# Scores on VectorE in one instruction per head, with paired score matmuls, a four-piece first weight unit and values by token tile

## The chip, the cores and the metric

The kernel runs on one core of a Trainium2 chip. The metric is the device time of one execution in microseconds (us), the median of several runs. The core has TensorE (PE, matrix products; PEld is its weight load), VectorE (DVE), ScalarE (ACT), GpSimd (POOL) and SyncE (SP), which issues the DMA transfers. Each engine works through its own instructions in order and waits on semaphores for the others.

## What is computed

A network of ten stages on 256 tokens of width 1024 in fp32: attention and MLP (layer 0), a state-space mixer and MLP (layer 1), and then twice a gated feed-forward, a mixer with differential attention and a causal convolution, and a second feed-forward. What the change touches is the softmax of the two attentions of layer 0 and of the two differential attentions. Cut to that:

```python
def windowed_gqa_sink(q, k, v, sink):       # attention "A": 8 query heads, 2 key heads
    s = einsum(qb, kb) * HEAD_DIM ** -0.5
    s = where(valid, s, NEG_INF)             # a band of 128 tokens
    p = softmax(concatenate([s, sink]))[..., :-1]
    return einsum(p, vb)

def neighborhood_attention(q, k, v, rpb):   # attention "B": 8 heads, a bias per head
    s = einsum(q_r, k_blk) * scale
    s = where(mask, s + bias, NEG_INF)
    return einsum(softmax(s), v_blk)

def diff_attention(q, k, v, rel_bias, lam, lam_init, subln_g):   # 4 heads x 2 maps, causal
    s = einsum(qi, k) * scale + bias
    p = softmax(where(dist >= 0, s, -1e30))
    a = p[:, :, 0] - lam * p[:, :, 1]
    return rms_norm(einsum(a, v), subln_g) * (1.0 - lam_init)
```

## The kernel before

The 256 tokens are two token tiles of 128 (`t` = 0, 1). Activations lie in SBUF in transposed form; an fp32 product is made of three fp32r matmuls, from a high part and a rest of both factors: names ending in `h` or `hh` are high parts, `l` or `hl` the rests. Only the key and value projections and the attention part of the output projection of the differential layers run as exact fp32 matmuls, straight from the weight buffer `st`. A matmul of fp32 operands (these, the scores `sc`, the products `po`) counts as two instructions in the trace. Weights come as 270 packed units of 1 MB through `unit` (L736) into three buffers `st`; ACT casts each half to `wh` (128x1024) and DVE subtracts to get `wl`. SP issues every transfer, in its order.

**The order.** The code does not issue its instructions directly. A `Recorder` keeps each operation with a priority (its number in the code plus the offsets of the table `BIAS` and of `rec.prio`), an estimated cost and its predecessors; `schedule` (L329) simulates the five engines and picks for each the ready operation of lowest priority; `issue` then writes all of them out from one line, L546, which is therefore the line of nearly every row of the trace. So an edit of a cost, of the order in the code or of the number of operations can move the instructions around it on every engine. Behind the scheduler each engine's order is fixed.

**The start.** `load_x` brings X in four pieces of 256 KB (token tile 0, columns 0 and 512; then tile 1), `first_T` transposes them (`tr<-ident,X`) to `xhl`, and `up` (L777) multiplies by the first unit (keys and values of A, `parts=FIRST_PARTS`, with `t_outer` all of tile 0 before tile 1). That unit is loaded in `FIRST_PARTS` = 2 pieces of 512 KB. `warm` runs 16 matmuls on a constant before.

**Attention of layer 0.** `attn` (L1153) runs `heads(t, part)` for part 0 (A) of both tiles, then, after the projections `up_T` for B, part 1 (B) of both tiles. `heads` calls `softmax_pair` (L1131) four times: for head pair (a, j) it takes a bank `sc`, computes two heads' scores with keys and queries on 64 partitions (rows 0 to 63 of the array for j = 0, rows 64 to 127 for j = 1), and then does, for both heads at once on DVE, `s = sc * 0.125 + bias` (SCALAR_TENSOR_TENSOR, 128x512), the maximum (TENSOR_REDUCE) and the negated maximum `nmx`; A's takes the minimum with `nsink` in the same small instruction. ACT makes exp with `nmx` as its bias per head and sums it; PE transposes the result (`tr<-ident,s`), which is copied to `pt` and multiplied by the values (`po`). A has 8 such pairs and B has 8. The acc rows beside B's scores are the output projection of A's result (`acc<-wh,hh` and so on).

**Differential layers.** `diff` works like that in its own `heads(t)`: four score banks for each tile, by (a, m), of two heads `u` each; tile 0 sees 128 keys (heads of 128x128), tile 1 sees 256. The three DVE steps per bank, exp on ACT, then on DVE `drd` (reciprocal), `dcc` and four `s<-s,dcc` that subtract the second map, transposes on PE (`ptps`), copies `pt`, products with the values `po`, a norm (`dss`, with a power on POOL, and `on`), transposes of `on`, copies `hd`, and the output projection `acc<-st,hd`. Beside all that DVE works off a causal convolution of 31 taps, the instructions `y<-ut,dprep,y` (120 of 128x256 per layer), whose result `hh`, `hl` is the other half of the output projection. The values are projected by `up([(W, 2048, 512)])`, 16 exact matmuls over the 8 slices of x, both tiles for each slice (`up<-st,x`).

Of the kernel before, what the change touches and what calls it, by code (L numbers as in the profile page):

```python
# [10 lines left out]
F32 = mybir.dt.float32  # L11
F32R = mybir.dt.float32r
AF = mybir.ActivationFunctionType
ALU = mybir.AluOpType
# [605 lines left out]
FIRST_PARTS = 2  # L620
# [59 lines left out]
class Net:  # L680
# [55 lines left out]
    def unit(self, srcs, a, exact=False, parts=1):  # L736
# [7 lines left out]
        for i in range(parts):  # L744
            nc.sync.dma_start(out=st[:, i * n:(i + 1) * n], in_=src[:, i * n:(i + 1) * n])
# [4 lines left out]
        for i in range(2):  # L750
# [5 lines left out]
            nc.scalar.copy(hv, s)  # L756
            nc.vector.tensor_tensor(lv, s, hv.bitcast(F32), op=ALU.subtract)
# [19 lines left out]
    def up(self, segs, t_outer=False, exact=False, parts=1):  # L777
# [20 lines left out]
        if t_outer:  # L798
            for t in range(2):
                for k in range(KM):  # L800
                    do(k, wk[k], t)
# [329 lines left out]
    def softmax_pair(self, t, a, j, q, k, bias, nmx, sums, nsink, s, pt):  # L1131

        nc = self.nc
        ps = self.bank([128, 2, T], "sc")
        pr = slice(64 * j, 64 * j + 64)
        for m in range(2):
            nc.tensor.matmul(ps[:, m], q[pr, 2 * a + m, t * 128:(t + 1) * 128], k(m)[pr], start=True, stop=True)
        nc.vector.scalar_tensor_tensor(s, ps, ATTN_SCALE, bias, op0=ALU.mult, op1=ALU.add)
        h2 = slice(4 * a + j, 4 * a + j + 3, 2)
        mx = self.tiny([128, 2], "mx")  # L1140
        nc.vector.tensor_reduce(mx, s, axis=AX.X, op=ALU.max)
        if nsink is not None:
            nc.vector.scalar_tensor_tensor(nmx[:, h2], mx, -1.0, nsink[:, h2], op0=ALU.mult, op1=ALU.min)
        else:
            nc.vector.tensor_scalar(nmx[:, h2], mx, -1.0, None, op0=ALU.mult)
        for m in range(2):
            h = 4 * a + j + 2 * m
            nc.scalar.activation(s[:, m], s[:, m], AF.Exp, bias=nmx[:, h:h + 1], accum_out=sums[:, h:h + 1])
# [4 lines left out]
    def attn(self, finish_of):  # L1153
        nc, I = self.nc, self.I
        W, Wo = Mat("attn_w_in", 0), Mat("attn_w_out", 0)
        with self.rec.phase_pool(name="attn", bufs=1) as ap:
# [18 lines left out]
            for t in range(2):  # L1175
                qn = nat()
                self.rope(ap, c, ps[t], 8, t, [qn.rearrange("p (h d) -> p h d", h=8)])
                self.transposes(qT[0][:, :, t * 128:(t + 1) * 128], qn, 4, nc.scalar.copy)

            def heads(t, part):  # L1180
# [3 lines left out]
                for a in range(2):  # L1184
                    s2 = self.w4([128, 2, 2, T], "s")
                    pt2 = self.w4([128, 2, 2, 2, 128], "pt")
                    for j in range(2):
                        if part == 0:
                            bias = c["band"][:, t].unsqueeze(1).to_broadcast([128, 2, T])
                            k = lambda m: kA[:, a]  # L1190
                        else:
                            e0 = 2 - 2 * t
                            bias = c["bt"][:, 4 * a + j:4 * a + j + 3:2, e0:e0 + 4].rearrange("p h e k -> p h (e k)")
                            k = lambda m: kB[:, 2 * a + m]
                        pt = self.softmax_pair(t, a, j, qT[part], k, bias, nmx, sums, c["nsink"] if part == 0 else None, s2[:, j], pt2[:, j])
# [653 lines left out]
```

## Time and profile before

| | |
|---|---|
| time, median of 3 runs | 1671.87 us (1671.65 to 1675.98) |
| the profiled execution | 1673.98 us |
| its span | 1672.2 us |
| PE busy | 1652.7 us (99%) |
| PEld busy | 1391.9 us (83%) |
| DVE busy | 1199.1 us (72%) |
| ACT busy | 924.0 us (55%) |
| POOL busy | 49.1 us (3%) |
| HBM read | 302.44 MB, 182 GB/s over the span |

The span is what the trace covers; 1.78 us of the profiled execution's time lie outside it. A row of the timeline gives the start, the time from first start to last end of a run of like instructions, the engine, the operation with its output and inputs, the shape, the count, and in brackets how long the engine had waited ahead of it and for what. Rows of successive instructions overlap a little, so the cost of an instruction in a chain is the distance from its start to the next start, and is smaller than its duration.

### The profile page before, as it was taken

The page shows a single profiled execution, that of the slowest core. Times are in us where ns is not written, and L with a number is a line of the kernel's source. Part 1 is how long each engine was busy: PE and PEld are TensorE (multiplying, and loading weights), DVE is VectorE, ACT ScalarE, POOL GpSimd, SP SyncE. Part 2 cuts the span into 40 slices and gives each one's busy share as a digit, 9 for nine tenths or more (in the row PEclk, how much of TensorE's full clock was granted, in tenths as well). Part 3 has the DMA queues.
Part 4 walks back from the last instruction along what each step waited for, and adds up shares of the span by engine and source line. Part 5 has one row for each costly group of instructions (what it writes and reads, how often), then busy time and mean ns, then how long its engine had stood idle before and what let it go on. Part 6 is the DMA issues. An engine that isn't in the chain of part 4 may idle for free.

```text
span 1672.2 us, 22864 instructions
## 1 busy us (share of the span) xinstructions
PE 1652.7 (99%) x8854; PEld 1391.9 (83%) x8854; DVE 1199.1 (72%) x1902; ACT 924.0 (55%) x1696; POOL 49.1 (3%) x50
## 2 busy tenths in 40 slices
PE   8999999999999999999999999999999999999999
PEld 7888888899987888888888658888888887578887
DVE  6767665999998666686665988665666658977652
ACT  5654444599995444465544257554455443566551
POOL 0000000000001000000000100000000001100000
PEclk9999999999999999999999999999999999999999
DMA  7535564384454556475554128555455532267540
GB/s 274 202 109 201 181 223 178 131 306 160 166 191 175 202 181 221 151 264 205 198 193 159 52 110 302 212 180 213 152 207 196 193 128 96 101 254 250 200 151 25
DMA packets 45694, 305.04 MB, mean 182 GB/s; under 512 B 5073, under 2 KB 5265, under 8 KB 11281
## 3 DMA queue, kind: packets, MB, share of 16 engines
q1 hardware_dynamic: 45584, 303.58, 49.8%
q8 instruction: 69, 1.13, 0.3%
q14 instruction: 41, 0.33, 0.1%
HBM read 302.44 MB, written 1.11 MB: 182 GB/s over the span
## 4 chain that ended last, share of the span: by engine, by line
PE 48%; DVE 7%; POOL 1%; issue 0%; ACT 0%; POOLq 0%; DVEq 0%
PE upW L546 24%; PE acc L546 17%; PE up L546 6%; DVE y L546 4%; PE tr L546 1%; POOL qr L546 1%; DVE s L546 1%; DVE dnmx L546 1%; DVE wl L546 0%; DVE X L546 0%; POOL rs L546 0%; DVE hn L546 0%; PE upT L546 0%; DVE nat L546 0%; PE ms L546 0%
## 5 line engine op out<-in xcount | busy, mean ns | idle before, releaser
L546 DVE TENSOR_TENSOR wl<-st,wh 128x1024 fp32r<-128x1024 f32 x516 | 623.0, 1219 | 220.4 <-PE upW L546 113.0
L546 ACT CAST wh<-st 128x1024 fp32r<-128x1024 f32 (+1 forms) x516 | 529.5, 1048 | 329.9 <-PE upW L546 167.5
L546 PE MATMUL upW<-xhl,wh 128*128 128x512 f32 x1600 | 403.4, 390 | 0.0
L546 PEld LDWEIGHTS upW<-xhl,wh 128*128 128x128 f32 x1600 | 297.5, 188 | 59.7
L546 PE MATMUL acc<-wh,hh 128*128 128x512 f32 x736 | 288.1, 394 | 0.0
L546 PE MATMUL acc<-wl,hh 128*128 128x512 f32 x736 | 287.5, 392 | 0.0
L546 PE MATMUL acc<-wh,hl 128*128 128x512 f32 x736 | 261.6, 392 | 0.0
L546 PE MATMUL up<-wh,xhl 128*128 128x512 f32 (+2 forms) x704 | 221.0, 386 | 3.6 <-ACT xhl L546 3.2
L546 PEld LDWEIGHTS upW<-xhl,wl 128*128 128x128 f32 x1600 | 205.3, 191 | 7.8
L546 PE MATMUL upW<-xhl,wl 128*128 128x256 f32 x1600 | 208.5, 283 | 0.0
L546 PEld LDWEIGHTS acc<-wh,hh 128*128 128x128 f32 x736 | 138.3, 188 | 29.0 <-issue 0.8
L546 PEld LDWEIGHTS acc<-wh,hl 128*128 128x128 f32 x736 | 138.2, 188 | 29.0 <-DVE hl L546 0.5
L546 PEld LDWEIGHTS acc<-wl,hh 128*128 128x128 f32 x736 | 138.5, 188 | 28.0 <-issue 1.4
L546 PEld LDWEIGHTS up<-wh,xhl 128*128 128x128 f32 x704 | 130.6, 190 | 28.7 <-ACT xhl L546 3.7
L546 PE MATMUL upT<-xhl,wh 128*128 128x256 f32 x736 | 138.9, 287 | 0.0
L546 PE MATMUL up<-wl,xhl 128*128 128x512 f32 (+2 forms) x352 | 136.1, 387 | 0.0
L546 PEld LDWEIGHTS upT<-xhl,wh 128*128 128x128 f32 x736 | 116.0, 191 | 1.6 <-issue 0.5
L546 PE MATMUL upT<-xhl,wl 128*128 128x256 f32 x368 | 104.9, 285 | 0.0
L546 DVE SCALAR_TENSOR_TENSOR y<-ut,dprep,y 128x256 f32<-128x256 f32 x240 | 98.5, 487 | 0.0
L546 PEld LDWEIGHTS up<-wl,xhl 128*128 128x128 f32 x352 | 66.7, 190 | 11.4
L546 PEld LDWEIGHTS upT<-xhl,wl 128*128 128x128 f32 x368 | 70.4, 191 | 0.3 <-issue 0.2
L546 DVE TENSOR_TENSOR r<-r,upW 128x256 f32<-128x256 f32 x56 | 23.2, 418 | 55.3 <-ACT r L546 55.3
(214 smaller groups left out, 1480.6 us busy)
## 6 DMA issues: line engine op xcount, KB each, us to landing
st<-in_pack SPq DMA_DIRECT2D x267, 1024.0 KB, 4.8
ar<-a_rows SPq DMA_DIRECT2D x16, 512.0 KB, 9.2
gv<-in_ln_g SPq DMA_DIRECT2D x4, 512.0 KB, 6.7
gv<-in_ln_b SPq DMA_DIRECT2D x4, 512.0 KB, 7.4
gv<-in_ffn_norm SPq DMA_DIRECT2D x4, 512.0 KB, 5.7
rpb_bt<-in_rpb_rows SPq DMA_DIRECT2D x1, 1536.0 KB, 8.0
st<-in_pack SPq DMA_DIRECT2D x2, 640.0 KB, 3.8
X<-in_x SPq DMA_DIRECT2D x4, 256.0 KB, 5.5
```

The source lines that it names most:

```text
L546: fn(*[real(a) for a in o.args], **{k: real(v) for k, v in o.kw.items()})
```

## The change

1. **Scores.** The three DVE steps of a pair become, for each head, one `tensor_tensor_reduce`: it writes `-(sc + bias)` to `s` and its minimum (in A together with the head's `nsink`) to `nmx`. The compiled program has two DVE instructions for it, `ISA s,nmx<-sc,...` of 128x256 (128x128 in tile 0 of the differential layers) and `ISA nmx` of 128x1, which fetches the accumulated value. Exp gets `scale=-1.0`. The factor 0.125 moves into the copies of the queries (an activation with a scale where a copy stood) and, in the differential layers, into `q_norm` (one tiny instruction per layer).
2. **Score pairs.** `scores` takes two banks and issues the score matmuls of a pair of banks alternately, one of row half 0, one of row half 1; `diff` does so as well.
3. **First unit.** `FIRST_PARTS` goes from 2 to 4: pieces of 256 KB, with priorities `FIRST_LATE`; casts and subtractions of this unit in halves (128x512); its matmuls by piece of two slices.
4. **Values by token tile.** In `diff` the values use `t_outer=True`, and the attention part of the output projection runs all of tile 0 and then all of tile 1.

PE's multiset of instructions stays the same; DVE goes from 1904 to 1940 instructions in the program, ACT from 1514 to 1516, SP from 319 to 321. The core of the diff:

```diff
-FIRST_PARTS = 2
+FIRST_PARTS = 4
+FIRST_LATE = (-45.5, -46.4, -46, -46)
...
         n = a * b // parts
         for i in range(parts):
-            nc.sync.dma_start(out=st[:, i * n:(i + 1) * n], in_=src[:, i * n:(i + 1) * n])
+            with self.rec.prio(FIRST_LATE[i] if parts > 1 else 0):
+                nc.sync.dma_start(out=st[:, i * n:(i + 1) * n], in_=src[:, i * n:(i + 1) * n])
...
-            nc.scalar.copy(hv, s)
-            nc.vector.tensor_tensor(lv, s, hv.bitcast(F32), op=ALU.subtract)
+            step = max(1, half // max(1, parts // 2))
+            for k in range(0, half, step):
+                ks = slice(k, k + step)
+                nc.scalar.copy(hv[:, ks], s[:, ks])
+                nc.vector.tensor_tensor(lv[:, ks], s[:, ks], hv[:, ks].bitcast(F32), op=ALU.subtract)
...
+        if parts > 1:
+            step = KM // parts
+            mm = self.nc.tensor.matmul
+            for t in range(2):
+                sl, o = slice(t * 128, (t + 1) * 128), ps[t][:, 0:n]
+                for k0 in range(0, KM, step):
+                    for p, (x, i) in enumerate(((self.xh, 0), (self.xl, 0), (self.xh, 1))):
+                        for k in range(k0, k0 + step):
+                            mm(o, x[:, k, sl], wk[k][i], start=k == 0 and p == 0, stop=k == KM - 1 and p == 2)
...
+    def scores(self, t, a, q, k):
+        pss = [self.bank([128, 2, T], "sc") for _ in range(2)]
+        for m in range(2):
+            for j, ps in enumerate(pss):
+                pr = slice(64 * j, 64 * j + 64)
+                self.nc.tensor.matmul(ps[:, m], q[pr, 2 * a + m, t * 128:(t + 1) * 128], k(m)[pr], start=True, stop=True)
+        return pss
...
-        nc.vector.scalar_tensor_tensor(s, ps, ATTN_SCALE, bias, op0=ALU.mult, op1=ALU.add)
-        h2 = slice(4 * a + j, 4 * a + j + 3, 2)
-        mx = self.tiny([128, 2], "mx")
-        nc.vector.tensor_reduce(mx, s, axis=AX.X, op=ALU.max)
...
         for m in range(2):
             h = 4 * a + j + 2 * m
-            nc.scalar.activation(s[:, m], s[:, m], AF.Exp, bias=nmx[:, h:h + 1], accum_out=sums[:, h:h + 1])
+            nc.vector.tensor_tensor_reduce(s[:, m], ps[:, m], bias[:, m], -1.0,
+                                           3e38 if nsink is None else nsink[:, h:h + 1], ALU.add, ALU.min,
+                                           accum_out=nmx[:, h:h + 1])
+            nc.scalar.activation(s[:, m], s[:, m], AF.Exp, bias=nmx[:, h:h + 1], scale=-1.0, accum_out=sums[:, h:h + 1])
...
-                self.transposes(qT[0][:, :, t * 128:(t + 1) * 128], qn, 4, nc.scalar.copy)
+                self.transposes(qT[0][:, :, t * 128:(t + 1) * 128], qn, 4,
+                                lambda o, p: nc.scalar.activation(o, p, AF.Copy, scale=ATTN_SCALE))
...
-                        nc.vector.scalar_tensor_tensor(sv, sc[:, :, 0:kn], ATTN_SCALE, self.t5[:, 2 * a:2 * a + 2, T - kn:T],
-                                                       op0=ALU.mult, op1=ALU.add)
-                        mx = nmx[:, m, 2 * a:2 * a + 2]
-                        nc.vector.tensor_reduce(mx, sv, axis=AX.X, op=ALU.max)
-                        nc.vector.tensor_scalar(mx, mx, -1.0, None, op0=ALU.mult)
                         for u in range(2):
                             h = 2 * a + u
-                            nc.scalar.activation(sv[:, u], sv[:, u], AF.Exp, bias=nmx[:, m, h:h + 1],
+                            mx = nmx[:, m, h:h + 1]
+                            nc.vector.tensor_tensor_reduce(sv[:, u], sc[:, u, 0:kn], self.t5[:, h, T - kn:T], -1.0, 3e38,
+                                                           ALU.add, ALU.min, accum_out=mx)
+                            nc.scalar.activation(sv[:, u], sv[:, u], AF.Exp, bias=mx, scale=-1.0,
                                                  accum_out=sums[:, m, h:h + 1])
...
-            ps = self.up([(W, 2048, 512)], exact=2 in EXACT_QKV)
+            ps = self.up([(W, 2048, 512)], t_outer=True, exact=2 in EXACT_QKV)
...
-            self.down(acc, self.items(hd, 4), Wo, True)
+            items = self.items(hd, 4)
+            ws = [w for i in (0, 2) for w in self.down_weights(Wo, items[i][2], items[i][0][1] is None)]
+            for t in range(2):
+                for i, ((h, k, _), w) in enumerate(zip(items, ws)):
+                    self.down_mm(acc, h, k, w, t, i == 0, False)
```

SP at the start; `st<-in_pack 128x1024` is a piece of 512 KB, `128x512` one of 256 KB, as is each X. Before:

```order
L546 DMA ident<-in_c_ident 128x128
L546 DMA X<-in_x 128x512 x2
L546 DMA st<-in_pack 128x1024 x2
L546 DMA X<-in_x 128x512 x2
L546 DMA st<-in_pack 128x2048 x2
L546 DMA asmall<-in_attn_small 128x648
```

After:

```order
L546 DMA ident<-in_c_ident 128x128
L546 DMA X<-in_x 128x512
L546 DMA st<-in_pack 128x512 x2
L546 DMA X<-in_x 128x512
L546 DMA st<-in_pack 128x512 x2
L546 DMA X<-in_x 128x512 x2
L546 DMA st<-in_pack 128x2048
L546 DMA asmall<-in_attn_small 128x648
```

The second piece of X now stands behind the first two pieces of the unit, and `asmall` (cosines, band, sink) ahead of the third unit instead of behind it. On PE the first `up` still comes behind eight transposes of X, that is behind both pieces of tile 0, but then as a run of nine of these matmuls instead of one.

PE in part A of the attention, from the scores on; `tr<-ident,s` are transposes of exp's result. Before:

```order
L546 MATMUL sc<-kA,qT_372 128x256 x4
L546 MATMUL tr<-ident,nat 128x128 x4
L546 MATMUL sc<-kA,qT_372 128x256 x12
L546 MATMUL upT<-xhl,wh 128x256
L546 MATMUL upT<-xhl,wl 128x256
```

After:

```order
L546 MATMUL sc<-kA,qT_385 128x256 x4
L546 MATMUL tr<-ident,nat 128x128 x4
L546 MATMUL sc<-kA,qT_385 128x256 x4
...
L546 MATMUL sc<-kA,qT_385 128x256
L546 MATMUL tr<-ident,s 128x128 x2
L546 MATMUL sc<-kA,qT_385 128x256
L546 MATMUL tr<-ident,s 128x128 x2
L546 MATMUL sc<-kA,qT_385 128x256
L546 MATMUL tr<-ident,s 128x128 x4
L546 MATMUL sc<-kA,qT_385 128x256
```

Sixteen score matmuls in two runs are now eight in two runs, four single ones among transposes, and four in two pairs further back.

PE in part B, up to the values' projection (the next row of both is `up<-wh,xhl`). Before:

```order
L546 MATMUL sc<-kB,qT_633 128x256 x6
...
L546 MATMUL tr<-ident,s 128x128 x2
L546 MATMUL sc<-kB,qT_633 128x256
L546 MATMUL tr<-ident,s 128x128 x2
L546 MATMUL sc<-kB,qT_633 128x256
L546 MATMUL tr<-ident,s 128x128 x2
L546 MATMUL sc<-kB,qT_633 128x256
L546 MATMUL tr<-ident,s 128x128 x2
L546 MATMUL sc<-kB,qT_633 128x256
L546 MATMUL tr<-ident,s 128x128 x4
```

After:

```order
L546 MATMUL sc<-kB,qT_613 128x256 x7
...
L546 MATMUL tr<-ident,s 128x128 x12
L546 MATMUL sc<-kB,qT_613 128x256 x5
...
L546 MATMUL tr<-ident,s 128x128 x10
L546 MATMUL sc<-kB,qT_613 128x256 x4
L546 MATMUL tr<-ident,s 128x128 x2
```

Of the sixteen score matmuls before, six stood singly between two transposes (four of them in the rows shown, two behind a later run of four); now they stand in runs of 7, 5 and 4, with 24 transposes ahead of the projection instead of 20, and 12 acc matmuls in both orders.

DVE and PE in a differential layer (both layers read alike), from the first score instruction on. DVE before:

```order
L546 SCALAR_TENSOR_TENSOR y<-ut,dprep,y 128x256 x6
L546 SCALAR_TENSOR_TENSOR s<-sc,t_bt 128x2x128 x3
L546 TENSOR_REDUCE dnmx<-s 128x2
L546 SCALAR_TENSOR_TENSOR s<-sc,t_bt 128x2x128
L546 TENSOR_SCALAR dnmx<-dnmx 128x2
L546 TENSOR_REDUCE dnmx<-s 128x2
L546 SCALAR_TENSOR_TENSOR s<-sc,t_bt 128x512
...
L546 SCALAR_TENSOR_TENSOR s<-s,dcc 128x128 x4
```

DVE after (eight heads of 128x128, one tap, eight heads of 128x256; of each the first rows):

```order
L546 SCALAR_TENSOR_TENSOR y<-ut,dprep,y 128x256 x6
L546 ISA s,dnmx<-sc,t_bt 128x128
L546 ISA dnmx 128x1
...
L546 SCALAR_TENSOR_TENSOR y<-ut,dprep,y 128x256
L546 ISA s,dnmx<-sc,t_bt 128x256
L546 ISA dnmx 128x1
...
L546 RECIPROCAL drd<-dsums 128x8
L546 SCALAR_TENSOR_TENSOR y<-ut,dprep,y 128x256
L546 SCALAR_TENSOR_TENSOR dcc<-dsums,dprep,drd 128x4
L546 SCALAR_TENSOR_TENSOR y<-ut,dprep,y 128x256
L546 SCALAR_TENSOR_TENSOR s<-s,dcc 128x128 x4
```

All sixteen heads, of tile 1 as well, and three taps now stand ahead of the four `s<-s,dcc` that PE's first `ptps` wait for; before, part of tile 1's maxima came behind them. PE before:

```order
L546 MATMUL sc<-kTd,qTd 128x128 x8
L546 MATMUL sc<-kTd,qTd 128x256 x8
L546 MATMUL up_8887<-st,x_8431 128x512
L546 MATMUL up_8876<-st,x_8442 128x512
L546 MATMUL up_8887<-st,x_8442 128x512
L546 MATMUL up_8876<-st,x_8442 128x512
L546 MATMUL up_8887<-st,x_8442 128x512
L546 MATMUL ptps<-ident,s 128x128 x4
```

PE after:

```order
L546 MATMUL sc<-kTd,qTd 128x128 x8
L546 MATMUL sc<-kTd,qTd 128x256 x8
L546 MATMUL up_8852<-st,x_8418 128x512
L546 MATMUL up_8969<-st,x_8407 128x512 x3
L546 MATMUL ptps<-ident,s 128x128 x4
L546 MATMUL up_8969<-st,x_8407 128x512
L546 MATMUL up_8969<-st,x_8418 128x512
L546 MATMUL po<-vd,pt 128x128 x4
```

Four of the values' matmuls instead of five now lie between the scores and the first `ptps`, and five instead of four behind them.

## Rows read from the trace of the kernel before

**Rows 1.** The page: busy time, share of the span and instructions of each engine.

```profile
PE 1652.7 (99%) x8854; PEld 1391.9 (83%) x8854; DVE 1199.1 (72%) x1902; ACT 924.0 (55%) x1696; POOL 49.1 (3%) x50
```

**Rows 2.** Timeline of the start: start, us, engine, operation, count [wait].

```profile
9.02 1.04 ACT L546 CAST wh<-st 128x1024 fp32r<-128x1024 f32 x1 [7.00 <-DMA st<-in_pack]
...
10.60 0.39 PE L546 MATMUL up<-wh,xhl 128*128 128x256 f32 x1 [3.21 <-ACT xhl L546]
```

**Rows 3.** Windows: us, PE, PEld, DVE, ACT, POOL busy, clock, DMA, GB/s.

```profile
10.60:12.00 1.40, 1.39 (x7) 1.19 (x8) 1.40 (x3) 1.40 (x3) 0.00 (x0) 0.78 1.04 436
12.00:14.00 2.00, 2.00 (x12) 2.00 (x11) 2.00 (x3) 1.06 (x2) 0.00 (x0) 0.50 1.01 426
14.00:15.00 1.00, 1.00 (x7) 1.00 (x7) 0.85 (x2) 0.87 (x1) 0.00 (x0) 0.60 1.00 397
33.70:57.15 23.45, 21.82 (x185) 20.17 (x185) 23.23 (x46) 17.68 (x48) 0.00 (x0) 1.00 0.35 124
```

**Rows 4.** Timeline of PE in part A.

```profile
42.60 0.44 PE L546 MATMUL tr<-ident,s 128*128 128x128 f32 x2 [1.29 <-ACT s L546]
```

**Rows 5.** Timeline of PE in part B.

```profile
72.41 1.99 PE L546 MATMUL sc<-kB,qT 64*128 64x256 f32 x12
...
77.31 0.70 PE L546 MATMUL sc<-kB,qT 64*128 64x256 f32 x2
77.94 0.44 PE L546 MATMUL tr<-ident,s 128*128 128x128 f32 x2
78.31 0.70 PE L546 MATMUL sc<-kB,qT 64*128 64x256 f32 x2
...
82.21 1.14 PE L546 MATMUL sc<-kB,qT 64*128 64x256 f32 x8
...
85.27 0.66 PE L546 MATMUL tr<-ident,s 128*128 128x128 f32 x4
85.69 0.48 PE L546 MATMUL up<-wh,xhl 128*128 128x512 f32 x1
```

**Rows 6.** Timeline of DVE in part A.

```profile
36.84 0.69 DVE L546 SCALAR_TENSOR_TENSOR s<-sc,asmall 128x512 f32<-128x512 f32 x1
37.44 0.15 DVE L546 SCALAR_TENSOR_TENSOR nmx<-mx,nsink 128x2 f32<-128x2 f32 x1
37.51 0.69 DVE L546 TENSOR_REDUCE mx<-s 128x2 f32<-128x512 f32 x1
```

**Rows 7.** Timeline of DVE in a differential layer.

```profile
959.10 2.45 DVE L546 SCALAR_TENSOR_TENSOR y<-ut,dprep,y 128x256 f32<-128x256 f32 x6
961.47 1.08 DVE L546 SCALAR_TENSOR_TENSOR s<-sc,t_bt 128x256 f32<-128x256 f32 x3
...
962.79 0.41 DVE L546 SCALAR_TENSOR_TENSOR s<-sc,t_bt 128x256 f32<-128x256 f32 x1
963.12 0.16 DVE L546 TENSOR_SCALAR dnmx<-dnmx 128x2 f32<-128x2 f32 x1
...
968.92 1.13 DVE L546 SCALAR_TENSOR_TENSOR s<-s,dcc 128x128 f32<-128x128 f32 x4
969.97 0.17 DVE L546 TENSOR_SCALAR dnmx<-dnmx 128x2 f32<-128x2 f32 x1
```

**Rows 8.** Timeline of ACT in part A.

```profile
48.27 0.49 ACT L546 ACTIVATE s<-s,nmx 128x256 f32<-128x256 f32 x1
48.67 0.19 ACT L546 ACTIVATION_READ_ACCUMULATOR s<-s,nmx 128x1 f32 x1
```

**Rows 9.** Timeline of PE in a differential layer.

```profile
963.87 4.56 PE L546 MATMUL up<-st,x 128*128 128x512 f32 x10
969.41 1.02 PE L546 MATMUL ptps<-ident,s 128*128 128x128 f32 x4 [0.99 <-DVE s L546]
...
976.34 2.05 PE L546 MATMUL po<-vd,pt 128*128 128x128 f32 x16 [0.56 <-DVE pt L546]
979.01 1.02 PE L546 MATMUL tr<-ident,on 128*128 128x128 f32 x4 [0.62 <-DVE on L546]
```

More of the change, by code (lines that the diff above doesn't have):

```diff
@@ L619 @@
 GAMMA_AHEAD = 200
-FIRST_PARTS = 2
+FIRST_PARTS = 4
+FIRST_LATE = (-45.5, -46.4, -46, -46)
+X_SECOND = 0
 WARM = 16
@@ L797, in up @@
                     do(k0 + i, w, t)
-        if t_outer:
+        if parts > 1:
[7 more added lines that the diff above has]
+                            mm(o, x[:, k, sl], wk[k][i], start=k == 0 and p == 0, stop=k == KM - 1 and p == 2)
+        elif t_outer:
             for t in range(2):
@@ L1129, in rope, with softmax_pair @@
             nc.vector.tensor_tensor(ov[:, :, 1], m1[:, :, 1], m2[:, :, 1], op=ALU.add)
-    def softmax_pair(self, t, a, j, q, k, bias, nmx, sums, nsink, s, pt):
-        nc = self.nc
[L1134 to L1137, printed above, removed]
-        nc.vector.scalar_tensor_tensor(s, ps, ATTN_SCALE, bias, op0=ALU.mult, op1=ALU.add)
-        h2 = slice(4 * a + j, 4 * a + j + 3, 2)
-        mx = self.tiny([128, 2], "mx")
-        nc.vector.tensor_reduce(mx, s, axis=AX.X, op=ALU.max)
[L1142 to L1145, printed above, removed]
+    def scores(self, t, a, q, k):
[5 more added lines that the diff above has]
+        return pss
+    def softmax_pair(self, ps, a, j, bias, nmx, sums, nsink, s, pt):
+        nc = self.nc
         for m in range(2):
             h = 4 * a + j + 2 * m
-            nc.scalar.activation(s[:, m], s[:, m], AF.Exp, bias=nmx[:, h:h + 1], accum_out=sums[:, h:h + 1])
+            nc.vector.tensor_tensor_reduce(s[:, m], ps[:, m], bias[:, m], -1.0,
+                                           3e38 if nsink is None else nsink[:, h:h + 1], ALU.add, ALU.min,
+                                           accum_out=nmx[:, h:h + 1])
+            nc.scalar.activation(s[:, m], s[:, m], AF.Exp, bias=nmx[:, h:h + 1], scale=-1.0, accum_out=sums[:, h:h + 1])
         self.transposes(pt.rearrange("p a b c -> p (a b) c"), s.rearrange("p a b -> p (a b)"), 4,
@@ L1186, in heads @@
                     pt2 = self.w4([128, 2, 2, 2, 128], "pt")
+                    pss = self.scores(t, a, qT[part], (lambda m: kA[:, a]) if part == 0 else (lambda m: kB[:, 2 * a + m]))
                     for j in range(2):
@@ L1193, in heads @@
                             bias = c["bt"][:, 4 * a + j:4 * a + j + 3:2, e0:e0 + 4].rearrange("p h e k -> p h (e k)")
-                            k = lambda m: kB[:, 2 * a + m]
-                        pt = self.softmax_pair(t, a, j, qT[part], k, bias, nmx, sums, c["nsink"] if part == 0 else None, s2[:, j], pt2[:, j])
+                        pt = self.softmax_pair(pss[j], a, j, bias, nmx, sums, c["nsink"] if part == 0 else None, s2[:, j], pt2[:, j])
                         for m in range(2):
@@ L1224, in attn @@
                 for i in range(2):
-                    nc.scalar.copy(d[:, 2 * i:2 * i + 2], self.up_T(W, col + 256 * i))
+                    nc.scalar.activation(d[:, 2 * i:2 * i + 2], self.up_T(W, col + 256 * i), AF.Copy,
+                                         scale=ATTN_SCALE if col == 768 else 1.0)
             hd = [heads(t, 1) for t in range(2)]
@@ L1499, in diff_prep @@
             nc.vector.tensor_scalar(sub, sm[:, o + 134:o + 262], 1.0 - li, None, op0=ALU.mult)
+            nc.vector.tensor_scalar(sm[:, o + 132:o + 133], sm[:, o + 132:o + 133], ATTN_SCALE, None, op0=ALU.mult)
             cT = [sm[:, o + 33 * i:o + 33 * i + 33] for i in range(4)]
```

10 lines of the change are left out of this document (5 added, 5 removed).

## The prediction

> **What bounds the kernel now.** I read the page first: PE is busy 99% of the span [rows 1], so the time can fall only where PE waits, where one of its instructions is dear because of what stands beside it, or at a low clock. The order on PE is fixed once the program is built, and the change keeps PE's set of instructions. So I looked for PE's waits in the four places where its order changes: the start, parts A and B of the attention, and each of the two differential layers.
>
> At the start PE stands 3.21 us before its first `up`; ACT had first to cast a 512 KB piece of the weight, which reached it at 9.02 [rows 2]. [...] In part A (33.70 to 57.15) DVE is busy 23.23 of 23.45 us and PE 21.82, so PE idles 1.63 in all [rows 3]; 1.29 of that is one wait for an exp [rows 4], which stands behind DVE's maxima. In part B PE hardly waits, but pays for single score matmuls: one costs 0.63 among transposes (from 77.31 to 77.94) [rows 5]. In a differential layer the waits around the softmax come to 0.99, 0.56 and 0.62 [rows 9], and DVE's chain ahead of the first runs without a gap from 961.47 to 969.97, 8.50 us [rows 7].
>
> **One head on DVE.** From start to start a 128x512 instruction takes 0.60 and a small one 0.07 [rows 6], so a pair costs 2 x 0.60 + 0.07 = 1.27. The trace has no combined instruction. The nearest row for its size and operands (one from PSUM, one from SBUF) is the 128x256 `s<-sc,t_bt`, 0.33 from start to start [rows 7]; for fetching the accumulator it is the small 0.07. That gives 0.40 per head, 0.80 per pair. A pointer as scalar adds 0.06: the tap `y`, also 256 wide, takes (961.47 - 959.10) / 6 = 0.395 [rows 7]; part A pays that for `nsink`, so 0.92 per pair. In tile 0 of the differential layers a head is 128 wide; with a pointer 128 elements take (969.97 - 968.92) / 4 = 0.26 [rows 7], without it 0.20, so 0.27 per head. Bounds: the fetch depends on the instruction right ahead of it, and may have to wait until that has run out; a 128x512 row lasts 0.69 against a distance of 0.60 [rows 6], so 0.09 more, 0.49 per head. If elements of the combined instruction pass at half the rate, it costs as one of 512 elements, 0.60 + 0.07 = 0.67. It can't be under 0.33, the price of the elements alone. I take 0.40. DVE then saves 8 x 0.35 + 8 x 0.47 = 6.6 us in the attention, but only what PE waits for counts.
>
> **Start.** Four of X's and the unit's 256 KB pieces (X, two of the unit, X) now land ahead of the first `up`, as many bytes as before, so its last input comes at about 9.0 as well. Before, this was the weight, and a cast of 1.04 (9.02 to 10.06) and the split of X came behind it on ACT; now it is X's second piece, and what is behind it is four transposes (two instructions of those take 0.37 when alone [rows 5], so 0.6) on PE itself, while the weight's casts and X's first split lie in the wait for that piece. First `up` at about 9.6 instead of 10.60: **1.0 us**. The later X pieces, the second unit and `asmall` are queued as many bytes deep as before or less, except for the third unit, which goes 0.3 MB further back, at the 426 GB/s of that stretch [rows 3] 0.8 us; `up` on that unit is several us behind. If PE is bound by landing pieces all the same, it is 0 to -0.5. If the shorter wait leaves the clock up, what the low clock costs comes back as well: 1.4 x 0.22 + 2 x 0.50 + 1 x 0.40 = 1.7 [rows 3], so up to 2.7. I leave the clock as it was, since the wait only shrinks from 3.2 to some 2.2 us.
>
> **Part A.** DVE's 2.8 us shorten the stretch by no more than PE's idle 1.6 [rows 3]. Against that, four scores now stand singly among transposes, each at 0.63 instead of 1.14 / 4 = 0.29 in a run [rows 5], and the pair of transposes behind it at 0.37 instead of 0.21 (half of 85.27 to 85.69): 4 x 0.5 = 2.0, less what the transposes paid before when single `upT` stood between them, some 0.1 for each of four. Net 1.6 - 1.6 = **0**, with bounds -1.5 (PE still waits for exps, since the order asks for them earlier) and +1.6 (the singles cost nothing).
>
> **Part B.** From 72.41 to 85.69 are 13.28 us [rows 5]. The scores take 1.92 (12 instructions; 74.33 is where the next begins, from the row's 1.99 less overlap) + 6 x 0.63 + 1.07 = 6.8; in runs of 7, 5 and 4, at 0.27 (1.07 / 4), they take 4.3: 2.5 less. Twenty transposes took 6 x 0.37 + 2 x 0.42 = 3.1; 24 in long runs at 0.105 take 2.5, and 4 are then done that came later: 1.0 less. New waits: twelve transposes ask for six exps at 0.49 [rows 8] and a copy of like length, 3.4 us on ACT, that start about 1 us behind the first score, while PE comes to them after seven scores and six acc, 1.9 + 1.4 = 3.3 us: about 1 us is waited. Gain **2.5**; bounds 1.5 (a cast of 1.04 lies between the exps) and 3.5 (no wait).
>
> **Differential layers, each.** DVE ahead of the first `ptps`: 8 x 0.27 + 8 x 0.40 + 3 taps x 0.395 + reciprocal and `dcc` 0.2 + four `s` 1.05 = 7.8 instead of 8.50, so `ptps` starts 0.7 earlier. PE has only four exact matmuls ahead of it instead of five, (969.41 - 0.99 - 963.87) / 5 = 0.91 each [rows 9], so its wait grows from 0.99 to about 1.2. But the fifth now covers the two later waits (0.56 and 0.62) which were uncovered: up to 0.9 of them goes. What is next late is `on` and `hd`, which I leave in part: 0.7 + 0.9 - 0.6 = **1.0**. The taps finish no later, since DVE has 16 cheaper heads in front of them. Bounds: at 0.49 a head the chain grows by 16 x 0.09 = 1.4, giving -0.4; at 0.33, +2. The values by token tile cost nothing by themselves: same instructions, same units, both loaded ahead.
>
> **The sum.** 1.0 + 0 + 2.5 + 2 x 1.0 = 5.5 us. The profiled run would go from 1673.98 (span 1672.2, 1.78 outside) to 1668.5. The median of the runs is 2.11 below the profiled one, so 1671.87 - 5.5 = **1666.4**.
>
> **Rivals.** (b) The clock stays up at the start: 1.7 more, 1664.7. For it: the idle time ahead of the first `up` shrinks by a third; against: over 2 us of it remain, and the clock fell behind 3.2. (c) The fetch waits for its instruction (0.49 per head): -0.4 in each differential layer instead of 1.0, and part A loses 1: 5.5 - 2.8 - 1 = 1.7 less than now, 1670.2. For it: rows are longer than their distances; against: ACT's exp, which has a fetch behind it as well, lasts 0.49, and the fetch starts 0.40 behind its start [rows 8], so that one doesn't wait for it to run out. (d) Slower: the combined instruction runs its elements at half the rate, 0.67 per head. Then a head of 256 costs 0.27 more than forecast and one of 128 0.13 more (half of it): each differential layer gets 8 x 0.40 = 3.2 later, -2.2; part A becomes longer on DVE, 2 x 0.73 - 1.27 = 0.19 by 8 pairs, -1.5; B keeps 1.0, since DVE needs 16 x 0.67 = 10.7 us there; the start keeps 1.0. Sum -3.9: 1675.8. It decides from about 0.16 per head above 0.40 (5.5 of the 9.4 us that 0.27 cost), where the layers eat what start and B gain. [...] (e) The pairs don't overlap on PE, and scores stay dear where halves alternate: B gains 0.5, 1668.4. Against it: in the run of 8 instructions, with halves in turn by twos, one costs 0.14, less than half of a single's 0.31 [rows 5].
>
> **Chances.** Forecast 0.50 (alone 1664 to 1669), (b) 0.15, (c) 0.22, (d) 0.08, (e) 0.05. A measurement tells about 0.3% (5.0 us) from no change: faster by more needs under 1666.9. More than half of the forecast's own range and nearly all of (b) lie there, about 0.45; (d) reaches beyond 1676.9 in less than half, 0.04; the rest is 0.51. The range holds all but (d): 1661.5 to 1672, the low end being (b) with part A's +1.6 and B's upper bound.
>
> **What would show it.** The first `up` near 9.6 with clocks as above; a head's `ISA` rows at 0.33 and 0.07 from start to start; part A as long as before, with singles among transposes; part B's stretch from first score to `up` at some 10.8 us; first `ptps` 0.7 us earlier after the scores. The forecast is wrong if a head costs over 0.5, if A's transposes wait over 1.5 us, or if `hh` comes late at the end of a differential layer.

## The result and the profile after

The changed kernel takes 1664.33 us (median of 5 runs, 1663.46 to 1666.12); the kernel before, timed beside it, 1673.26 (1671.65 to 1679.18). The ratio is 0.9941 with a 95% interval of 0.9926 to 0.9957, so 8.9 us or 0.59% faster; against the 1671.87 from which the forecast counted, 7.5 us. The forecast was 5.5 us less, 1666.4, with a range of 1661.5 to 1672. The profiled runs stand at 1673.98 before and 1663.46 after, their spans at 1672.2 and 1661.7: 10.5 us.

First the page of after (to be held against [rows 1]):

```profile
PE 1647.8 (99%) x8854; PEld 1388.6 (84%) x8854; DVE 1184.1 (71%) x1938; ACT 924.8 (56%) x1698; POOL 50.9 (3%) x50
```

PE has the same 8854 instructions and is busy 4.9 us less: about half of the gain isn't a wait that went but instructions that took less time (a part of it at the start, where the clock stayed up, see below). To place the rest I read the start of the same row in both timelines: the first score of A, the first score of B, the next `up` behind B's scores, the first score of a differential layer, and the first `up` of the next stage.

| stretch | before | after | gain | forecast |
|---|---|---|---|---|
| start, up to A's first score | 33.73 | 31.59 | 2.1 | 1.0 |
| part A, up to B's first score | 38.68 | 38.37 | 0.3 | 0 |
| part B, up to the next `up` | 13.28 | 10.57 | 2.7 | 2.5 |
| between B and the state-space layer | 52.32 | 51.87 | 0.4 | in B |
| differential layer 0, first score to next `up` | 48.25 | 46.34 | 1.9 | 1.0 |
| differential layer 1, the same | 48.24 | 46.40 | 1.8 | 1.0 |
| projections ahead of the two layers' scores | 22.80, 22.81 | 22.26, 22.33 | 1.0 | 0 |

The last line is not the change's: in the profiles of the experiments below it reads either about 22.25 or about 22.8 with one and the same order, in step with the power on POOL that the query norm waits for (two of them took 4.15 us in the profile of before, 3.61 in that of after). Where the clock stays at 1.00, all the other lengths behind the start come back within 0.1 us in every profile of an equal order (the layers of after and of after_first2: 46.34 and 46.36, 46.40 and 46.38), so one profile is enough to compare them; stretches with a fallen clock do not (below). One thing in the table is not like for like: with four pieces seven `upT` matmuls of part A stand ahead of A's first score instead of behind it. after_first2 has them in part A, its other instructions there stand in the order of after, and it takes 39.21, 0.84 more. For the same work the start gained 3.0 in this pair of profiles and part A lost 0.5.

DVE in a differential layer of after (compare [rows 7]): the combined instruction and its fetch have names of their own here.

```profile
955.29 0.29 DVE L546 CUSTOM_DVE_ANT_0 s<-sc,t_bt 128x128 f32<-128x128 f32 x1
955.50 0.09 DVE L546 DVE_READ_ACCUMULATOR2_ANT dnmx<- 128x1 f32 x1
955.50 0.29 DVE L546 CUSTOM_DVE_ANT_0 s<-sc,t_bt 128x128 f32<-128x128 f32 x1
...
957.38 0.42 DVE L546 CUSTOM_DVE_ANT_0 s<-sc,t_bt 128x256 f32<-128x256 f32 x1
957.72 0.09 DVE L546 DVE_READ_ACCUMULATOR2_ANT dnmx<- 128x1 f32 x1
957.72 0.42 DVE L546 CUSTOM_DVE_ANT_0 s<-sc,t_bt 128x256 f32<-128x256 f32 x1
...
961.13 1.14 DVE L546 SCALAR_TENSOR_TENSOR s<-s,dcc 128x128 f32<-128x128 f32 x4
962.18 0.48 DVE L546 SCALAR_TENSOR_TENSOR y<-ut,dprep,y 128x256 f32<-128x256 f32 x1
```

A head of 256 costs 0.34 from start to start, one of 128 costs 0.21. The fetch starts where the next head starts (957.72), so it costs here at most the 0.01 by which 0.34 exceeds the 0.33 of the nearest row of before [rows 7].

PE in part B of after (compare [rows 5]):

```profile
69.96 1.99 PE L546 MATMUL sc<-kB,qT 64*128 64x256 f32 x14
...
73.38 1.77 PE L546 MATMUL tr<-ident,s 128*128 128x128 f32 x12
75.08 1.56 PE L546 MATMUL sc<-kB,qT 64*128 64x256 f32 x10
...
78.07 1.28 PE L546 MATMUL tr<-ident,s 128*128 128x128 f32 x10
79.27 1.13 PE L546 MATMUL sc<-kB,qT 64*128 64x256 f32 x8
80.34 0.44 PE L546 MATMUL tr<-ident,s 128*128 128x128 f32 x2
80.53 0.48 PE L546 MATMUL up<-wh,xhl 128*128 128x512 f32 x1
```

No row has a wait. Ten score instructions take 1.49 (75.08 to 76.57, where an acc begins), 0.15 each, where a single matmul of two took 0.63.

### The profile page after: what moved, and what is told of

The parts are those of the page before. It is cut to its first block, busy times and chain, and to the rows that moved or that the text cites. A ratio compares the mean times of both kernels' runs of the same rounds, so it can differ in the third digit from the quotient of the medians.

```text
span 1661.7 us, 22901 instructions
## 1 busy us (share of the span) xinstructions
PE 1647.8 (99%) x8854; PEld 1388.6 (84%) x8854; DVE 1184.1 (71%) x1938; ACT 924.8 (56%) x1698; POOL 50.9 (3%) x50
## 4 chain that ended last, share of the span: by engine, by line
PE 51%; DVE 4%; POOL 1%; ACT 1%; issue 0%; POOLq 0%; DVEq 0%
PE upW L546 24%; PE acc L546 16%; PE up L546 8%; DVE y L546 1%; PE upT L546 1%; PE tr L546 1%; DVE wl L546 1%; DVE s L546 0%; ACT s L546 0%; DVE X L546 0%; POOL rs L546 0%; POOL qr L546 0%; POOL dss L546 0%; DVE hn L546 0%; ACT nat L546 0%
## 5 line engine op out<-in xcount | busy, mean ns | idle before, releaser
L546 DVE TENSOR_TENSOR wl<-st,wh 128x1024 fp32r<-128x1024 f32 (+1 forms) x518 | 622.7, 1214 | 224.0 <-PE upW L546 113.5
```

Of the source, the lines that this page charges most:

```text
L546: fn(*[real(a) for a in o.args], **{k: real(v) for k, v in o.kw.items()})
```

## The experiments

Twelve kernels ran. A short diff says what each changes; "after" and "before" are the two kernels of this document. The stretches are read as in the table above.

**after_threesteps**: the three DVE steps per pair put back, all else as after.

```diff
-            nc.vector.tensor_tensor_reduce(s[:, m], ps[:, m], bias[:, m], -1.0, ..., ALU.add, ALU.min, accum_out=...)
+        nc.vector.scalar_tensor_tensor(s, ps, ATTN_SCALE, bias, op0=ALU.mult, op1=ALU.add)
+        nc.vector.tensor_reduce(mx, s, axis=AX.X, op=ALU.max)
+        nc.vector.tensor_scalar(nmx[:, h2], mx, -1.0, None, op0=ALU.mult)
```

> The kernel after with the three DVE steps per pair put back (score pairs, pieces and token order stay). Theory 1 (the shorter DVE chain makes the gain in B and in the differential layers): the stretch of B from first score to up goes from 10.6 to 12.5 us or more, since single scores among transposes come back, first ptps in the differential layers waits 1.3 us longer after the scores; in all about 5 us slower than after. Theory 2 (the score pairs and the token order make it): under 1.5 us slower.

Measured: 1669.41 us, ratio to before 0.9975 (0.9963 to 0.9986), 5.1 us slower than after. B 12.54, between B and the state-space layer 52.80, a differential layer 47.67 and 47.63, first `ptps` 9.63 us behind the first score instead of 7.27. Theory 1 holds in sum, though `ptps` comes 2.4 us later behind the scores, not 1.3, and part A is 0.6 shorter than in after (37.73).

**after_nopairs**: the scores bank by bank, all else as after.

```diff
-                    for u in range(2):
-                        for m, sc in enumerate(scs):
+                    for m in range(2):
+                        sc = self.bank([128, 2, T], "sc")
+                        for u in range(2):
```

(the same in the attention's `scores`).

> The kernel after with the scores issued bank by bank. Theory 1: its B still has runs of 6, 4, 4 and 2 scores, so B is at most 0.5 us longer than 10.6; the scores of a differential layer take 3.4 instead of 3.1 us; in all about 1.2 us slower than after. Theory 2 (pairs make B's gain): B over 12.5 us, in all about 3.5 us slower.

Measured: 1664.38 us, ratio 0.9944 (0.9932 to 0.9956): the same as after. But two opposite effects hide in it. Part A takes 38.85 (0.5 longer), B 11.73 (1.2 longer, more than theory 1's bound, less than theory 2's), and a differential layer 45.32 and 45.27, 1.1 us shorter than after where theory 1 had it longer.

**after_first2**: the first unit in two pieces again.

```diff
-FIRST_PARTS = 4
+FIRST_PARTS = 2
```

(with the casts, the order of the pieces and the first matmul loop of before).

> The kernel after with the first unit as before: two pieces of 512 KB, whole casts, matmuls slice by slice. Theory 1 (the clock makes most of the start's gain): PE waits over 3 us for its first up again, the granted clock falls to about 0.5 behind it, A's first score comes at about 33.7 us instead of 31.59, so 2.1 us slower than after; the other stages keep their lengths. Theory 2 (only the earlier first matmul counts, the clock has nothing to do with the pieces): about 1.0 us slower, clock at 1.0 throughout.

Measured: 1665.21 us, ratio 0.995 (0.9937 to 0.9963), 0.9 us slower than after; the two intervals overlap, so the times don't tell the two kernels apart. In its profile PE waited 2.09 us ahead of the first `up`, at 9.53, the clock stayed at 1.00, and A's first score came at 31.31, earlier than in after, but with seven `upT` fewer ahead of it; part A then takes 39.21, so that B's first score comes at 70.52 instead of 69.96. Neither theory fits that profile; see the start below.

**after_byslice**: values and output projection of the differential layers slice by slice again.

```diff
-            ps = self.up([(W, 2048, 512)], t_outer=True, exact=2 in EXACT_QKV)
+            ps = self.up([(W, 2048, 512)], exact=2 in EXACT_QKV)
...
-            for t in range(2):
-                for i, ((h, k, _), w) in enumerate(zip(items, ws)):
-                    self.down_mm(acc, h, k, w, t, i == 0, False)
+            self.down(acc, self.items(hd, 4), Wo, True)
```

> The kernel after with the values and the output projection of the differential layers slice by slice, as before. Theory 1 (the prediction's: this part costs and gives next to nothing): each differential layer at most 0.5 us longer, 1 us slower in all. Theory 2 (with values by token tile the products of tile 0 no longer wait for tile 1's values, and that is what exceeds the forecast there): 1.2 us or more per layer, 2.5 us in all.

Measured: 1675.6 us, ratio 1.0015 (1.0006 to 1.0024): 11 us slower than after and slower than before. A layer takes 51.63 and 52.93. Both theories are far too small. Its PE in layer 0:

```profile
967.38 2.84 PE L546 MATMUL po<-vd,pt 128*128 128x128 f32 x24
972.75 1.01 PE L546 MATMUL tr<-ident,on 128*128 128x128 f32 x4 [2.53 <-DVE on L546]
```

and the windows of that layer (stretch, its length, busy time of PE, PEld, DVE, ACT, POOL, granted clock, DMA share, GB/s):

```profile
970.00:975.00 5.00, 2.01 (x8) 0.88 (x7) 4.79 (x18) 3.55 (x13) 2.28 (x2) 1.00 0.33 139
975.00:980.00 5.00, 4.99 (x19) 4.06 (x19) 4.12 (x10) 2.33 (x6) 0.70 (x1) 0.50 0.19 26
980.00:985.00 5.00, 5.00 (x13) 2.70 (x13) 2.92 (x9) 3.87 (x10) 0.00 (x0) 0.82 0.46 187
```

All the values are done before `po`, so nothing is left on PE while the norm of `po` runs through POOL and DVE: 2.53 us of waiting, and a granted clock of 0.50 in the 5 us window behind it (975 to 980). PE's waits in the layer come to 3.06 in all, against 1.92 in after; its busy time goes from 44.42 to 48.57 in layer 0 and 49.89 in layer 1, at a mean granted clock of 0.93 and 0.90. In after_valslice, below, the two layers have these lengths and clocks the other way round, so 51.5 or 53 is a draw of the clock and not a matter of the layer.

**before_ttr**: the combined instruction alone, put into before.

```diff
+            nc.vector.tensor_tensor_reduce(s[:, m], ps[:, m], bias[:, m], -1.0, ..., ALU.add, ALU.min, accum_out=...)
```

> The kernel before with the combined DVE instruction alone (scores bank by bank, first unit in two pieces, values by slice). Theory 1: B's single scores go into runs (6, 4, 4, 2) by this part alone, the stretch from first score to up falls from 13.3 to about 11 us; the differential layers gain over 1 us each; in all 4 to 5 us faster than before. Theory 2 (the gain needs the pairs and the token order): under 2 us faster.

Measured: 1679.98 us, ratio 1.0038 (1.0026 to 1.0051). The change's name-giving part by itself makes the kernel slower. B gains as theory 1 said (11.73), but the layers take 51.56 and 53.03, with the same waits of 2.5 us for `on`. Both theories counted on a gain. One of the nine executions was granted a clock of 1.000 in the mean and took 1675.94; the other eight, at 0.993 to 0.996, took 1678.9 to 1682.38. By this one execution some 4 of the 7 us that the kernel lost are the clock's, and the rest is there without it.

**before_token** and **before_pairs**: part 4 alone and part 2 alone in before.

```diff
+            ps = self.up([(W, 2048, 512)], t_outer=True, exact=2 in EXACT_QKV)
```

> The kernel before with values and output projection by token tile alone. Theory 1: a differential layer within 0.5 us of before. Theory 2 (this part is what exceeds the forecast): over 1.2 us shorter per layer.

Measured: a layer 47.65 and 47.66, 0.6 us shorter than before, a little over theory 1's bound; one run, 1672.88 us.

```diff
+    for m in range(2):
+        for j, ps in enumerate(pss):
```

(and the same in `diff`).

> The kernel before with the score pairs alone. Theory 1: B keeps six single scores, so its stretch stays within 0.7 us of 13.3; the scores of a differential layer take 3.1 instead of 3.4 us but the first ptps waits for DVE all the same; under 1 us faster in all. Theory 2: B falls to about 11 us.

Measured: B 12.54 (0.7 shorter, at theory 1's bound), a layer 48.23 and 48.23 as before; one run, 1671.33 us. Theory 1.

**after_valslice**: only the values slice by slice, the output projection by token tile.

```diff
-            ps = self.up([(W, 2048, 512)], t_outer=True, exact=2 in EXACT_QKV)
+            ps = self.up([(W, 2048, 512)], exact=2 in EXACT_QKV)
```

> The kernel after with the values slice by slice again, the output projection still by token tile. Theory 1 (the values by token tile leave matmuls that cover the wait for on): PE waits about 2.5 us for on in each differential layer, the granted clock falls to 0.5 behind it, and a layer takes 51 to 53 us from its first score to the next up instead of 46.35. Theory 2 (the order of the output projection is what counts): 46 to 47 us.

Measured: two waits of 2.5 us for `on`, a layer 52.97 and 51.48. Theory 1: it is the values, not the output projection.

**byslice_fill**: after_byslice with each product `po` of token tile 1 done three times.

```diff
-                    for kt in range(t + 1):
+                    for kt in list(range(t + 1)) * (3 if t else 1):
                         nc.tensor.matmul(po[:, h], pts[h // 2][:, h % 2, kt], ...
```

> The kernel after with values and output projection slice by slice, where the products po of token tile 1 are each done three times (the result stays the same), which puts 16 more small matmuls, about 2 us of PE work per layer, where PE waited 2.5 us for on. Theory 1 (most of the loss is the low clock behind that wait): the wait shrinks below 1 us, the clock stays at 1.0, a layer takes about 48 us instead of 51.6 and 52.9, and the kernel is some 8 us faster than without the added work. Theory 2 (the wait itself is the loss): no faster, or slower by the added work.

Measured: 1670.8 us, ratio 0.9976 (0.9965 to 0.9988), against 1.0015 without the added work: 0.0039 of before's time or 6.5 us faster by doing more (4.8 between the two medians, 5.6 in the two layers of the profiles). A layer takes 49.48 and 49.46. PE and the windows of layer 0:

```profile
967.74 5.30 PE L546 MATMUL po<-vd,pt 128*128 128x128 f32 x46
973.12 0.30 PE L546 MATMUL tr<-ident,on 128*128 128x128 f32 x1
```

```profile
970.00:975.00 5.00, 4.91 (x43) 4.56 (x42) 4.89 (x16) 1.85 (x6) 1.11 (x1) 1.00 0.40 169
975.00:980.00 5.00, 4.97 (x20) 2.70 (x20) 2.92 (x5) 4.57 (x13) 2.36 (x2) 1.00 0.02 3
980.00:985.00 5.00, 4.43 (x17) 2.46 (x18) 4.72 (x15) 3.20 (x11) 0.10 (x1) 1.00 0.58 210
```

The wait of 2.53 is gone, the clock stays at 1.00 in the same stretches, and the layers end 2.2 and 3.5 us earlier although PE has 32 instructions more in each. That is theory 1, a little smaller than its 8 us. It won back 2.2 of the 5.3 and 3.5 of the 6.5 us that a layer of after_byslice is longer than one of after, with the added work to pay out of that, so the low clock is about half of that loss. The order behind it differs a little too, so this is not a pure test.

**before_warm22**: 22 warming matmuls in place of 16.

```diff
-WARM = 16
+WARM = 22
```

> The kernel before with 22 instead of 16 warming matmuls, which end at about 8.5 us, so that PE idles 1.3 instead of 3.2 us ahead of its first up; transfers and first up (10.6 us) as before. Theory 1 (idle time pulls the clock down, and that is most of the start's gain): the clock stays at 1.0 from 10.6 to 15 us and A's first score comes 1.5 to 2 us earlier than 33.73. Theory 2 (the clock falls for another reason, or what it costs is hidden by landing weights): A's first score within 0.5 us of 33.73.

Measured: the wait ahead of the first `up` is 1.08 us, the clock stays at 1.00, A's first score comes at 31.81, 1.9 earlier than in before: theory 1 at the start. Yet the run took 1675.57, since part A took 43.50 instead of 38.68. Its windows there:

```profile
38.00:42.00 4.00, 2.79 (x23) 2.35 (x23) 3.97 (x10) 2.79 (x12) 0.00 (x0) 1.00 0.00 0
42.00:44.00 2.00, 2.00 (x17) 2.00 (x15) 2.00 (x7) 1.62 (x6) 0.00 (x0) 0.67 0.27 49
44.00:52.00 8.00, 8.00 (x40) 8.00 (x40) 4.49 (x9) 5.07 (x15) 0.00 (x0) 0.50 0.29 120
52.00:54.00 2.00, 2.00 (x16) 2.00 (x16) 1.05 (x4) 0.53 (x2) 0.00 (x0) 0.77 0.00 0
```

Waits of 0.41 and 1.08 us for exps, of the same kind as in before [rows 4], were followed here by 8 us at a granted clock of 0.50 (44 to 52); in the profile of before they were not, part A reads 1.00 there [rows 3].

**after_diffbank** and **diffbank_runs8**: two attempts at something better. The first keeps the pairs in the attention and drops them in the differential layers; the second adds one line to the scheduler's table, so that the attention's scores go first.

```diff
     ('attn', 'po', 'PE'): 30,
+    ('attn', 'sc', 'PE'): -100,
```

> The kernel after with the differential layers' scores bank by bank again, the pairs of the attention kept. Theory 1 (the pairs help in B by 1.2 us and cost 1.0 us in each differential layer, since PE's order there then asks for crs before it is ready): from the first score of a layer to its next up 45.3 instead of 46.35 us, B stays at 10.6; about 2 us faster than after. Theory 2 (the two can't be had together, or the difference is one of single executions): within 0.5 us of after.

> The same as after with the differential scores bank by bank, and with a priority that puts the attention's score matmuls ahead (A and B each in two runs of eight, no single ones). Theory 1 (single scores among transposes cost PE 0.5 us each and nothing else bounds A): A 1.5 us shorter than 38.4, B about 10. Theory 2 (PE then waits for exps): A no shorter, with new waits on ACT of over 1 us, perhaps with a lower clock behind them.

Measured: after_diffbank 1661.89 us (1661.3 to 1662.17), ratio 0.9928 (0.9914 to 0.9942), 2.4 us under after (the two intervals overlap, but the layers of the profiles are 1.0 and 1.1 shorter each); B 10.58, a layer 45.35 and 45.27. diffbank_runs8 1659.49 us (1658.64 to 1660.74), ratio 0.9915 (0.99 to 0.9929), 2.4 us under that; A, B and what follows up to the state-space layer take 98.28 together instead of 100.76, with one wait of 0.16 us for an exp. Theory 1 in the first, and in sum in the second: there B's first scores moved up ahead of B's stretch, so that A and B apart can't be compared with the table's.

## Why the forecast came out as it did

The sign and the range were right, the size was 5.5 us where 8.9 were measured, and some of the reasons were wrong. That the measured 1664.33 lies beside rival (b)'s 1664.7 is luck: (b) adds to the forecast only the clock at the start, while the profiles have the two layers 1.7 us above the forecast and part A 0.5 below it.

**One head on DVE.** Taken at 0.40, bounded at 0.33 and 0.67; measured 0.34, at the lower bound, 0.40 with `nsink` (rows of part A at 33.16 and 33.56) and 0.21 for 128. The term that was mis-sized is the fetch: 0.07 was charged for it, and 0.34 against 0.33 leaves it at most 0.01. So DVE's chain ahead of the first `ptps` takes 6.9 us (955.29 to 962.18) where 7.8 were forecast, and `ptps` comes 1.7 us earlier behind the scores (8.98 to 7.27) instead of 0.7. Rivals (c) and (d) fall with that number. So does (e): a score instruction in B's runs costs 0.15, a single one 0.31. That elements pass at half the rate, from which (d) had its 0.67, was an assumption of the author's that no row here shows: a head of 256, with one source in PSUM and the accumulator, takes 0.34 against the 0.33 of the nearest row without accumulator.

**The differential layers.** Forecast 1.0, measured 1.9 and 1.8. The step that failed is that the forecast counted the 0.7 by which DVE's shorter chain brings `ptps` forward as a gain of its own, and that it gave the values by token tile no part beyond the matmul that they put behind `ptps` (they "cost nothing by themselves"). The shorter chain gains only together with them. All eight combinations of these three parts were run, read here from one profile each (the pieces of the first unit don't matter to a layer: after_first2 has 46.36 and 46.38):

| DVE steps | values | scores | layer 0, layer 1 |
|---|---|---|---|
| three | by slice | by bank (before) | 48.25, 48.24 |
| three | by slice | in pairs (before_pairs) | 48.23, 48.23 |
| three | by token tile | by bank (before_token) | 47.65, 47.66 |
| three | by token tile | in pairs (after_threesteps) | 47.67, 47.63 |
| combined | by slice | by bank (before_ttr) | 51.56, 53.03 |
| combined | by slice | in pairs (after_byslice) | 51.63, 52.93 |
| combined | by token tile | by bank (after_nopairs) | 45.32, 45.27 |
| combined | by token tile | in pairs (after) | 46.34, 46.40 |

The combined instruction makes a layer 3.3 to 4.8 us longer with the values by slice; with them by token tile it makes it 2.3 shorter with the scores by bank and 1.3 with the scores in pairs, as in after. In the first case the softmax is done so early that `po` follows in one run and PE has nothing left behind it but the wait for `on`; in the second the rest of tile 1's values covers it. PE in layer 0 of after (compare [rows 9]):

```profile
957.33 3.70 PE L546 MATMUL up<-st,x 128*128 128x512 f32 x8
961.53 1.11 PE L546 MATMUL ptps<-ident,s 128*128 128x128 f32 x4 [0.49 <-DVE s L546]
...
968.09 1.02 PE L546 MATMUL up<-st,x 128*128 128x512 f32 x2
969.91 0.30 PE L546 MATMUL tr<-ident,on 128*128 128x128 f32 x1 [0.80 <-DVE on L546]
...
971.94 4.46 PE L546 MATMUL acc<-st,hd 128*128 128x512 f32 x10
...
980.47 0.71 PE L546 MATMUL crs<-dg,ones 128*128 128x128 f32 x4 [0.63 <-DVE dg L546]
```

The forecast left a remainder of the waits standing; here it is 0.80 for `on`, and a new one that it didn't name, 0.63 for `dg`. PE's waits in the layer fall from 2.65 to 1.92, which is 0.7 of the 1.9. The other 1.2 is PE's busy time, 45.60 before and 44.42 after with the same instructions, a term that the forecast put at nothing: the scores take 3.07 from their first start to the next row instead of 3.44, the transposes of `on` 0.5 less. The pairs cost 1.1 us a layer in this combination: without them (after_nopairs) the waits are 0.96 for `s` and 0.26 for `on`, 1.2 in all against 1.9, and PE is busy 0.3 less (44.10).

**Part B.** Forecast 2.5, measured 2.7 and 0.4 behind it. The price of the scores was right (2.5 less forecast, 2.3 measured: 6.75 to 4.47), but a transpose in a long run costs 0.12 to 0.14 (12 from 73.38 to 75.08), not 0.105, so that 24 take as long as 20 did before, 3.05. The runs of scores come from two parts: the combined instruction alone brings B to 11.73 (before_ttr), the pairs alone to 12.54, both to 10.57. The wait of 1 us that the forecast charged didn't come, and so the two misses nearly cancel.

**Part A.** Forecast 0, and 0.3 in the table, but that is not the balance that was forecast. The windows of part A in before, after_first2 and after:

```profile
33.73:72.41 38.68, 37.05 (x312) 35.29 (x311) 32.47 (x55) 25.39 (x58) 0.00 (x0) 1.00 0.57 211
31.31:70.52 39.21, 39.21 (x311) 35.20 (x311) 29.14 (x63) 26.37 (x59) 0.00 (x0) 1.00 0.59 214
31.59:69.96 38.37, 38.37 (x304) 34.36 (x304) 28.15 (x62) 26.37 (x59) 0.00 (x0) 1.00 0.60 226
```

(The counts take in one or two instructions that began ahead of the stretch.) With the seven `upT` counted in, as in after_first2, part A got 0.5 us longer: PE's idle 1.6 went to nothing, as forecast, but its busy time rose by 2.2 (37.05 to 39.21), where the forecast charged 1.6 for the single scores. That is the term that was too small. after_threesteps bears it out: without the combined instruction part A is 0.6 shorter than in after, although PE idles 2.0 in it. PE in part A of after:

```profile
35.31 0.70 PE L546 MATMUL sc<-kA,qT 64*128 64x256 f32 x2
35.93 0.44 PE L546 MATMUL tr<-ident,s 128*128 128x128 f32 x2
36.30 0.70 PE L546 MATMUL sc<-kA,qT 64*128 64x256 f32 x2
```

From start to start the score takes 0.62 and the two transposes 0.37, as forecast from B. diffbank_runs8, where no score of A or B stands singly, gave 2.5 us over A, B and what follows.

**The start.** Rival (b)'s condition held in this profile: the clock stayed up. Its first rows and windows (compare [rows 2, 3]):

```profile
8.37 0.66 PE L546 MATMUL tr<-ident,X 128*128 128x128 f32 x4 [1.24 <-DMA X<-in_x]
8.83 0.51 PE L546 MATMUL up<-wh,xhl 128*128 128x256 f32 x2
```

```profile
10.60:12.00 1.40, 1.40 (x15) 1.40 (x14) 1.11 (x3) 0.75 (x3) 0.00 (x0) 1.00 0.95 398
12.00:14.00 2.00, 2.00 (x20) 2.00 (x19) 1.24 (x2) 0.96 (x2) 0.00 (x0) 1.00 1.06 432
```

The first `up` comes at 8.83 instead of the 9.6 that was forecast, since the wait for X's second piece lasted 1.24 us only. But how much of the gain is the four pieces differs from run to run. Of five profiles with two pieces and 16 warming matmuls (before, before_pairs, before_token, before_ttr, after_first2), the wait was 3.21, 2.19, 3.79, 2.72 and 2.09 us, the clock fell in the first, third and fourth, and A's first score came at 33.2 to 34.2 in those and at 31.3 and 31.9 in the others. Of eight with four pieces it fell in one (after_valslice, wait 2.32, A's first score at 33.78); the others are at 31.2 to 32.3. On the mean over these profiles the first `up` comes at 10.3 with two pieces and at 8.6 with four, A's first score at 32.9 and at 32.0, and with four pieces the seven `upT` (0.84 us) are done by then as well. So by the profiles the part is worth some 1.7 us on the mean, and the larger gain of the profile pair is in part two different draws of the clock. after_first2's times say 0.9, within the noise, so its size is known only as one to two us. The forecast's 1.0 was too small, since it had X's second piece arrive at about 9.0, and it took the clock as fixed where the clock varies between executions.

The times of before spread over 1671 to 1681 us in one set of 17 runs while those of after lie within 3. The clock that each execution was granted in the mean goes with it: in that set the four from 1678.24 to 1680.63 show 0.994 to 0.996, the thirteen up to 1676.08 show 0.999 or 1.000, and the five of after show 1.000. A fall at the start (2 us) or in part A (4.8 us, as in before_warm22) would do it; where it fell in those four was not traced, and why it falls in some executions and not in others stays open.

## What to carry to other kernels

When a chain on one engine gets shorter, the instructions that covered the next wait may be used up earlier; look for the wait that follows and for what is left to cover it. The 2.5 us waits on PE cost here about as much again by the clock of 0.50 behind them, so that even useless matmuls paid (byslice_fill: 2.2 and 3.5 us a layer). Run the parts of a change alone and left out, and compare by stretch: here one part loses 3.3 to 4.8 us a layer or gains 1.3 to 2.3 depending on another, and one that left the time as it was (the pairs in after) gained 1.6 us in the attention and lost some 2 in the layers. And before two stretches are compared, count what is in them: here seven matmuls had crossed the border.

## What the runs showed of the hardware

The accumulator's fetch on DVE starts together with the next instruction (957.72 in the rows above): a head costs 0.34 with it, and the nearest row without it 0.33, so that 16 of them in a layer add next to nothing to the chain. With the clock the same kind of wait (0.4 and 1.1 to 1.3 us for exps in part A) was followed by a granted clock of 0.50 in one profile (before_warm22, 8 us) and not in another (before, 1.00), with the same order in part A; and one kernel, before, was granted 1.000 in some executions and 0.994 in another. So what a short wait costs is not fixed by the kernel alone.
